# First tiles in halves, three issuing engines, and the constants behind the fifth tile, in a one-core hybrid encoder layer

## The chip, the cores and the metric

The kernel runs on one core of a Trainium2 chip. The metric is the device time of one execution in microseconds, as a median of several runs. The engines are TensorE (PE, with its weight loads as PEld), VectorE (DVE), ScalarE (ACT), GpSimd (POOL) and SyncE (SP, which issues most transfers). A row with "q" behind the engine (SPq, ACTq, POOLq) is the issue of a transfer.

## The reference

One layer for 512 positions of 1024 channels in float32. What the change touches is the very beginning: the norm, the input projection and the branch gates.

```python
def rms_norm(x, g):
    y = x32 * lax.rsqrt(jnp.mean(x32 * x32, axis=-1, keepdims=True) + EPS)
    return (y * g.astype(jnp.float32)).astype(x.dtype)
...
h = rms_norm(x, norm_mix[l])
proj = jnp.einsum('bsd,dc->bsc', h, w_in[l])
u_pool, u_lru, q, k, v, g_logits = jnp.split(proj, splits, axis=-1)
gates = jax.nn.sigmoid(g_logits + b_gate[l]).reshape(B, S, N_BRANCH, D_MODEL)
y_pool, y_lru = pool_mixer(u_pool, ...), rglru_mixer(u_lru, ..., lru_lambda[l])
y_sb = stick_breaking_attention(qh, kh, vh)      # after a norm of q and k by head
merged = (gates[:, :, 0] * jnp.einsum('bsc,cd->bsd', y_pool, w_branch[l, 0])
          + gates[:, :, 1] * jnp.einsum('bsc,cd->bsd', y_lru, w_branch[l, 1])
          + gates[:, :, 2] * jnp.einsum('bsc,cd->bsd', y_sb, w_branch[l, 2]))
x = x + jnp.einsum('bsd,de->bse', merged, w_out[l])
h2 = rms_norm(x, norm_ffn[l])
act = jax.nn.silu(h2 @ w_ffn_gate[l]) * (h2 @ w_ffn_up[l])
x = x + act @ w_ffn_down[l]
```

## The kernel before

Channels lie on the 128 partitions, positions (512) in the free dimension; the contraction of 1024 channels is done in eight tiles k of 128. Every float32 product is made of three matmuls: each operand is split into a rounded high part and the remainder, and high x high, high x low and low x high are added. Splitting takes a copy with rounding (on ScalarE, or a CAST on VectorE) and a subtraction on VectorE. For weights these parts are called `whi` and `wlo`, for the input `hu` holds both parts of x times the norm's weight (without the root of the mean square, which is applied later to the outputs).

The kernel begins with a gate projection of 512 columns. Its weights come as four `raw` tiles of two k each ("first", 0 to 3); `raw` has three buffers. `xt` is the transposed input, one tile of 128 x 512 for each k. Tile 0 of the weights is handled apart: `raw0` is loaded in two pieces, one for each k, and VectorE makes both parts (L451, L452). Tiles 1 to 3 go through `split_w` (ScalarE L111, VectorE L112). `make_h(k)` makes the parts of the input: ScalarE L437, VectorE L438, with the norm's weight taken as a column of `vt`. `vt` (128 x 114) holds every small constant of the layer, the norm's weights, biases and `lru_lambda` among them; it is loaded first. Meanwhile TensorE runs matmuls on a constant tile `warm` (L422). The gate matmuls are at L701: for each k, four column groups n for (whi, hu high), four for (wlo, hu high) and four for (whi, hu low).

`lru_constants` (L540 to L560) turns `lru_lambda` into two columns by a chain of some 25 tiny VectorE operations with one GpSimd power (L547) in it. `input_rms` loads the plain input `xs` and takes its squares on ScalarE. Both are written behind the first gate matmuls or later.

The order in which each engine's instructions stand is made by a scheduler from the program and its priorities, not by the written order alone: it is fixed at build time, and each engine has one list. A transfer also stands in the list of the engine that issues it, and waits there if the semaphore or buffer that it takes is not free.

Of the kernel before, what the change touches and what calls it, by code (L numbers as in the profile page):

```python
# [8 lines left out]
F32 = mybir.dt.float32  # L9
F32R = mybir.dt.float32r  # L10
BF16 = mybir.dt.bfloat16
AF = mybir.ActivationFunctionType
ALU = mybir.AluOpType
# [3 lines left out]
P = 128  # L17
S = 512
D = 1024
KT = D // P  # L20
# [4 lines left out]
HD = 128  # L25
QSCALE = float(HD) ** -0.5
EARLY = 300
WARM = 9
GBUFS = 27
NDIRECT = 2  # L30
KD = 10
NTICK = (1, 1)
H = S // 2
AHEAD = 200
PAD = 41


OFF = 16
# [11 lines left out]
VOFF = {}  # L50
# [17 lines left out]
def layer_kernel(ctx: ExitStack, tc: tile.TileContext, x, xt, vecs, w_in, w_qkv7, w_gate7, w_pool, w_rg, w_ig,  # L68
                 w_branch, w_br7, w_out, w_fg, w_fu, w_fd, w_fd7, out):
    nc = tc.nc  # L70
    act = nc.scalar.activation
    dve = nc.vector

    cst = ctx.enter_context(tc.tile_pool(name="cst", bufs=1))
# [18 lines left out]
    def cols(ap, k0, nk, c0, nc_):  # L93
        return ap[k0 * P:(k0 + nk) * P, c0:c0 + nc_].rearrange("(k p) c -> p k c", p=P)
# [5 lines left out]
    def weight_tiles(nh, nl, o=0):  # L100
        return [wp.tile([P, 1024 + 128], F32R, tag=tag, name=n)[:, o:o + 1024]
                for tag, n in (("whi", nh), ("wlo", nl))]
# [158 lines left out]
    def emit_next():  # L261
        i = state["i"]
        if i >= len(specs):
            return
        state["i"] = i + 1
        key, make = specs[i]
        with tc.high_priority(AHEAD if i > 6 else 0):
            ready[key] = make(str(i))

    def weights(*key):  # L270
        while key not in ready:
            emit_next()
        while len(ready) < 3 and state["i"] < state["stop"]:
            emit_next()
        return ready.pop(key)
# [16 lines left out]
    vt = cst.tile([P, NV], F32, tag="vt", name="vt")  # L292

    def vcol(name, i=0):
        o = VOFF[name] + i
        return vt[:, o:o + 1]


    cst.tile([P, PAD], F32, tag="pad", name="pad")
    warm = cst.tile([P, S], BF16, tag="warm", name="warm")  # L300
    dve.memset(warm, 1.0)
# [55 lines left out]
    def chunk_psum(key, pool, pair=False):  # L357
        nm = "ps_" + "_".join(map(str, key))
        if pool is None:
            return [pmm.tile([P, S], F32, tag="mm", name=nm + f"_{j}") for j in range(2)]  # L360
        t = pool.tile([P, 2, S], F32, tag="mm", name=nm)
        return t if pair else [t[:, j, :] for j in range(2)]


    def chan_chunk(key, rhs, nticks=0, pool=None, pair=False):
        pss = chunk_psum(key, pool, pair)
        for half in range(2):
            half_chunk(pss if type(pss) is list else [pss[:, j, :] for j in range(2)], key, half, rhs,
                       nticks)
        return pss  # L370
# [37 lines left out]
    with ExitStack() as first:  # L408
# [7 lines left out]
        def t4(shape, name, dt=F32):  # L416
            return b4(shape, name, "t", dt)


        wps = pb.tile([P, 2, S], F32, tag="mm", name="warm_ps")  # L420
        for i in range(WARM):
            nc.tensor.matmul(wps[:, 0, :], warm[:, 0:P], warm, start=True, stop=True)  # L422
# [4 lines left out]
        xts = [xp[k // 2][:, k % 2, :] for k in range(KT)]  # L427
        hu = []

        def load_xt(k):  # L430
            nc.sync.dma_start(xts[k], xt[k * P:(k + 1) * P, :])

        def make_h(k):
            t = t4([2, S], f"hu{k}", F32R)
            hh, hl = t[:, 0, :], t[:, 1, :]
            gcol = vcol("norm_mix", k)
            act(hh, xts[k], AF.Copy, scale=gcol)  # L437
            dve.scalar_tensor_tensor(hl, xts[k], gcol, hh.bitcast(F32), ALU.mult, ALU.subtract)  # L438
            hu.append((hh, hl))


# [1 line left out]
        hi0, lo0 = (t.rearrange("p (a b) -> p a b", a=2) for t in weight_tiles("whi0", "wlo0"))  # L443
        raw0 = wp.tile([P, 2, 512], F32, tag="raw", name="raw0")
        ready["first", 0] = hi0, lo0
        src0 = cols(w_in, 0, 2, 5120, 512)
        nc.sync.dma_start(vt, vecs)
        for k in range(2):
            load_xt(k)
            (nc.sync if k else nc.scalar).dma_start(raw0[:, k, :], src0[:, k, :])  # L450
            dve.tensor_copy(hi0[:, k, :], raw0[:, k, :])  # L451
            dve.tensor_tensor(lo0[:, k, :], raw0[:, k, :], hi0[:, k, :].bitcast(F32), ALU.subtract)  # L452
            make_h(k)
        load_xt(2)
        emit_next()
        make_h(2)
        load_xt(3)
        make_h(3)
        load_xt(4)
        emit_next()  # L460
        make_h(4)
        for k in range(5, KT):
# [11 lines left out]
        def input_rms():  # L474
            ssq = cst.tile([P, NS, 2], F32, tag="ssqa", name="ssqa")
            ms = cst.tile([P, NS], F32, tag="msa", name="msa")
            for sj in range(NS):
                t = w4([2, 512], f"xs{sj}")
                nc.sync.dma_start(t, x[sj * P:(sj + 1) * P, :].rearrange("p (e c) -> p e c", e=2))
                for ej in range(2):  # L480
                    act(t[:, ej, :], t[:, ej, :], AF.Square, accum_out=ssq[:, sj, ej:ej + 1])
            dve.tensor_tensor(ms, ssq[:, :, 0], ssq[:, :, 1], ALU.add)
            dve.tensor_scalar(ms, ms, 1.0 / D, EPS, ALU.mult, ALU.add)
            rsqrt(rx, ms, (NS,), "a")
# [210 lines left out]
        pss = [chunk_psum(("gate", 0, c), pb) for c in range(2)]  # L695
        for k in range(KT):
            if k % 2 == 0:
                wh, wl = weights("first", k // 2)
            for w, x_ in ((wh, 0), (wl, 0), (wh, 1)):
                for n in range(4):  # L700
                    nc.tensor.matmul(pss[n // 2][n % 2], w[:, k % 2, n * P:(n + 1) * P], hu[k][x_],  # L701
                                     start=k == 0 and w is wh and x_ == 0,
                                     stop=k == KT - 1 and x_ == 1)
            if k == 3:
                input_rms()
        bg.append(rms_broadcast)
# [146 lines left out]
        for cc in range(2):  # L853
# [14 lines left out]
            for nm in ORDER:  # L868
                ps, half, first_, t, ts_, src, ss = plan[nm]
# [314 lines left out]
    with ExitStack() as third:  # L1184
# [42 lines left out]
        for u, nm in BORDER:  # L1227
            z, half, first_, sn, ts_ = plan[nm]
# [5 lines left out]
            for w in range(2):  # L1234
                o = ps[:, w, half * H:(half + 1) * H]
                for k in range(4):
                    for n, (x_, y_) in enumerate(((0, 0), (0, 1), (1, 0))):
                        nc.tensor.matmul(o, ah[x_][:, w, k, :], b[k][y_], start=first_ and n == k == 0,  # L1238
                                         stop=n == 2 and k == 3, skip_group_check=True)
            if sn is not None:  # L1240
                if (u, sn) not in snaps:
                    snaps[u, sn] = ap2.tile([P, 2, S], F32, tag="t", name=f"bt{u}{sn}")
                with tc.high_priority(EARLY):
                    act(snaps[u, sn][:, :, ts_], ps[:, :, hi], AF.Copy,
                        scale=-1.0 if sn and (u, sn) in gated else 1.0)
# [10 lines left out]
    with ExitStack() as ffn:  # L1256
        gp = ffn.enter_context(tc.tile_pool(name="gp", bufs=GBUFS))

        def g4(shape, name, dt=F32):

            return gp.tile([P] + shape, dt, tag="g", name=name)
# [13 lines left out]
        for c in range(4):  # L1275
# [7 lines left out]
            pss = psh[c] if c < 2 else chan_chunk(("out", c), mt, pool=fp)  # L1283
            hh = g4([2, S], f"h2h{c}", F32R)
            hl = g4([2, S], f"h2l{c}", F32R)
            for j in range(2):
                k = 2 * c + j
# [5 lines left out]
                gcol = vcol("norm_ffn", k)  # L1293
# [272 lines left out]
        for e in range(2):  # L1566
            wh, wl = weights("fd", e)
# [4 lines left out]
            for j in range(4):  # L1572
                m = 4 * e + j
                cs = slice(j * P, (j + 1) * P)
# [117 lines left out]
```

## Time and profile before

| what | value |
|---|---|
| median of 3 runs | 898.24 us (898.1 to 898.4) |
| profiled execution, own time | 898.31 us |
| profiled execution, span | 896.5 us |
| TensorE busy | 891.2 us, 99% of the span |
| VectorE / ScalarE / GpSimd busy | 739.4 / 528.5 / 88.8 us |
| moved by DMA | 154.08 MB, mean 172 GB/s |

A row of the timeline has its start, its duration, engine, line, operation, output <- input, shapes, a count of merged instructions, and in brackets the idle time before it with what ended it. A row of the waits says who waited for whom: total, times, longest. A row of a stretch gives the busy time of TensorE, its weight loads, VectorE, ScalarE and GpSimd (instructions in brackets), the granted clock, the share of the DMA engines and their GB/s. A row of issues gives the size and the median time from issue to landing.

### The profile page before, as it was taken

How to read it: one execution, taken by the hardware profiler on the slowest of the kernel's cores; microseconds unless marked ns; L12 is line 12 of the kernel's file. 1: busy time of each engine (PE TensorE's matmuls, PEld its weight loads, DVE VectorE, ACT ScalarE, POOL GpSimd, SP SyncE). 2: the span in 40 equal slices, each digit the busy share in tenths (PEclk: the TensorE clock that was granted, in tenths of full speed). 3: DMA queues.
4: the chain of work that ended last, by engine and by line, in shares of the span. 5: the costliest groups of instructions: out<-in, count | busy, mean ns of one | idle time of the engine just before them, and what ended most of it. 6: DMA issues, size and time to landing. Idle time of an engine off the chain costs nothing.

```text
span 896.5 us, 14227 instructions
## 1 busy us (share of the span) xinstructions
PE 891.2 (99%) x5563; PEld 795.2 (89%) x5563; DVE 739.4 (82%) x934; ACT 528.5 (59%) x730; POOL 88.8 (10%) x130
## 2 busy tenths in 40 slices
PE   9999999999999999999999999999999999999998
PEld 6888778788889888888888988889999999999998
DVE  6897897997786599967887695699988888899974
ACT  6554989546856556554664544545555555746642
POOL 1110002222323101000001100000000000021200
PEclk9999999999999999999999999999999999999999
DMA  9495336798692785734636865336443343897913
GB/s 337 141 297 167 118 114 215 217 302 252 174 276 72 217 252 175 236 108 152 205 90 154 179 190 170 106 107 169 126 131 104 95 118 97 228 243 195 186 42 118
DMA packets 116644, 154.08 MB, mean 172 GB/s; under 512 B 8161, under 2 KB 90081, under 8 KB 116577
## 3 DMA queue, kind: packets, MB, share of 16 engines
q1 hardware_dynamic: 103904, 107.30, 37.8%
q0 software_dynamic: 12528, 45.62, 21.6%
q8 instruction: 43, 0.70, 0.3%
q10 hardware_dynamic: 144, 0.26, 0.1%
q14 instruction: 25, 0.20, 0.1%
HBM read 132.71 MB, written 18.87 MB: 169 GB/s over the span
## 4 chain that ended last, share of the span: by engine, by line
PE 95%; DVE 2%; ACT 2%; issue 1%; DMA 0%; SPq 0%; DVEq 0%; ACTq 0%
PE ps_y L287 11%; PE ps_x L287 8%; PE ps_q L798 7%; PE ps_dy L1611 6%; PE ps_dx L1611 5%; PE ps_br L278 3%; PE ps_br L279 3%; PE ps_br L280 3%; PE ps_bY L1238 2%; PE ps_gate L701 2%; PE ps_gy L287 2%; PE ps_gate L280 2%; PE ps_bX L1238 2%; PE ps_gx L287 2%; PE ps_gate L278 2%; PE ps_gate L279 2%
## 5 line engine op out<-in xcount | busy, mean ns | idle before, releaser
L111 ACT ACTIVATE whi<-raw 128x1024 fp32r<-128x1024 f32 x69 | 73.1, 1060 | 85.2 <-PE ps_out L279 17.9
L112 DVE TENSOR_TENSOR wlo<-raw,whi 128x1024 fp32r<-128x1024 f32 x69 | 84.4, 1223 | 30.7 <-ACT whi L111 30.7
L112 DVE TENSOR_TENSOR wlo<-qw,whi 128x1024 fp32r<-128x1024 f32 x48 | 58.6, 1224 | 22.0 <-ACT whi L111 21.8
L111 ACT ACTIVATE whi<-qw 128x1024 fp32r<-128x1024 f32 x48 | 50.7, 1059 | 33.2 <-PE ps_q L798 15.3
L1403 ACT ACTIVATE wh_S<-w_S 128x1024 fp32r<-128x1024 f32 x36 | 38.3, 1067 | 34.4 <-PE ps_y L287 22.3
L1404 DVE TENSOR_TENSOR wl_S<-w_S,wh_S 128x1024 fp32r<-128x1024 f32 x36 | 43.8, 1222 | 5.2 <-ACT wh_S L1403 5.1
L1515 POOL DMA_DIRECT2D dw<-in_w_down_dram x20 | 16.9, 847 | 313.6 <-DMA dw<-in_w_down_dram 253.2
L1403 ACT ACTIVATE wh<-w 128x1024 fp32r<-128x1024 f32 x27 | 28.8, 1067 | 30.2 <-issue 11.9
L1404 DVE TENSOR_TENSOR wl<-w,wh 128x1024 fp32r<-128x1024 f32 x27 | 33.0, 1222 | 9.9 <-ACT wh L1403 9.9
L1403 ACT ACTIVATE whdS<-dw 128x1024 fp32r<-128x1024 f32 x20 | 21.3, 1067 | 22.5 <-PE ps_dy L1611 11.0
L1404 DVE TENSOR_TENSOR wldS<-dw,whdS 128x1024 fp32r<-128x1024 f32 x20 | 24.3, 1226 | 6.5 <-ACT whdS L1403 6.4
L1054 DVE TENSOR_TENSOR_SCAN E<-K,ahead 128x512 f32<-128x512 f32 (+3 forms) x32 | 25.4, 815 | 4.4 <-ACT K L1050 4.4
L278 PE MATMUL ps_br<-yHH,whi 128*128 128x512 f32 x64 | 25.3, 395 | 0.0
L278 PE MATMUL ps_lru<-HH,whi 128*128 128x512 f32 x64 | 25.2, 394 | 0.0
L278 PE MATMUL ps_br<-yph,whi 128*128 128x512 f32 x64 | 25.2, 394 | 0.0
L278 PE MATMUL ps_pool<-HH,whi 128*128 128x512 f32 x64 | 25.2, 393 | 0.0
L280 PE MATMUL ps_gate<-HH,wlo 128*128 128x512 f32 x64 | 25.0, 391 | 0.0
L278 PE MATMUL ps_gate<-HH,whi 128*128 128x512 f32 x64 | 25.0, 391 | 0.0
L279 PE MATMUL ps_br<-ypl,whi 128*128 128x512 f32 x64 | 25.0, 391 | 0.0
L280 PE MATMUL ps_br<-yph,wlo 128*128 128x512 f32 x64 | 25.0, 391 | 0.0
L279 PE MATMUL ps_br<-yHL,whi 128*128 128x512 f32 x64 | 25.0, 390 | 0.0
L279 PE MATMUL ps_pool<-HL,whi 128*128 128x512 f32 x64 | 25.0, 390 | 0.0
(737 smaller groups left out, 3448.5 us busy)
## 6 DMA issues: line engine op xcount, KB each, us to landing
raw<-in_w_in_dram SPq DMA_DIRECT2D x31, 512.0 KB, 5.3
qw<-in_w_qkv_dram SPq DMA_DIRECT2D x24, 512.0 KB, 7.4
dw<-in_w_down_dram POOLq DMA_DIRECT2D x20, 512.0 KB, 7.5
w<-in_w_ffn_gate_dram SPq DMA_DIRECT2D x36, 256.0 KB, 4.0
w<-in_w_ffn_up_dram SPq DMA_DIRECT2D x36, 256.0 KB, 4.6
raw<-in_w_branch_dram SPq DMA_DIRECT2D x16, 512.0 KB, 4.1
qw<-in_w_qkv_dram POOLq DMA_DIRECT2D x12, 512.0 KB, 7.7
qd<-r POOLq DMA_DIRECT2D x12, 512.0 KB, 7.9
```

Source lines behind the costliest of these rows:

```text
L111: act(hi, raw, AF.Copy)
L112: dve.tensor_tensor(lo, raw, hi.bitcast(F32), ALU.subtract)
L278: nc.tensor.matmul(ps, lh, rh, start=start, stop=False, skip_group_check=skip)
L279: nc.tensor.matmul(ps, lh, rl, start=False, stop=False, skip_group_check=skip)
L280: nc.tensor.matmul(ps, ll, rh, start=False, stop=stop, skip_group_check=skip)
L287: nc.tensor.matmul(o, a_[a][:, w, k, :], b_[b][:, k, :], start=first and n == k == 0, stop=last and n == 2 and k == 3, skip_group_check=True)
L798: nc.tensor.matmul(ps[:, a, :], b_[:, k, ts_], a_[:, kk, :], start=first and n == k == 0, stop=n == 2 and k == 3, skip_group_check=True)
L1054: dve.tensor_tensor_scan(E[:, c0:c0 + n][:, ::-1], K[:, c0 + 1:c0 + n + 1][:, ::-1], ahead[:, S - n:][:, ::-1], 0.0, ALU.mult, ALU.add)
L1238: nc.tensor.matmul(o, ah[x_][:, w, k, :], b[k][y_], start=first_ and n == k == 0, stop=n == 2 and k == 3, skip_group_check=True)
L1403: act(h, src, AF.Copy)
L1404: dve.tensor_tensor(l, src, h.bitcast(F32), ALU.subtract)
L1611: nc.tensor.matmul(o, a_[a][:, w, k0 + k, :], b_[b][:, k, :], start=first and i == k == 0, stop=last and i == 2 and k == nk - 1, skip_grou ...
```

## The change

The norm's eight weight columns get a tile of their own, `nmix`, loaded first from the same array; the pad behind it shrinks by eight columns, so that the other constants keep their addresses. The first input tile and the first half of `raw0` are loaded in two column halves each, from SyncE and ScalarE; the second half of `raw0` (for k=1) is loaded whole, from GpSimd. The rounding of the weights, `make_h(0)` and the matmuls of k=0 work on halves too: 24 matmuls of 256 columns for 12 of 512. `vt` is loaded behind the fifth input tile. There are seven warming matmuls instead of nine.

```diff
-WARM = 9
+WARM = 7
-PAD = 41
+PAD = 33
+    nmix = cst.tile([P, 8], F32, tag="nmix", name="nmix")
...
-        def make_h(k):
+        def make_h(k, parts=(slice(0, S),)):
...
-            gcol = vcol("norm_mix", k)
-            act(hh, xts[k], AF.Copy, scale=gcol)
-            dve.scalar_tensor_tensor(hl, xts[k], gcol, hh.bitcast(F32), ALU.mult, ALU.subtract)
+            gcol = nmix[:, k:k + 1]
+            for ts_ in parts:
+                act(hh[:, ts_], xts[k][:, ts_], AF.Copy, scale=gcol)
+            for ts_ in parts:
+                dve.scalar_tensor_tensor(hl[:, ts_], xts[k][:, ts_], gcol, hh[:, ts_].bitcast(F32),
+                                         ALU.mult, ALU.subtract)
...
-        nc.sync.dma_start(vt, vecs)
-        for k in range(2):
-            load_xt(k)
-            (nc.sync if k else nc.scalar).dma_start(raw0[:, k, :], src0[:, k, :])
-            dve.tensor_copy(hi0[:, k, :], raw0[:, k, :])
-            dve.tensor_tensor(lo0[:, k, :], raw0[:, k, :], hi0[:, k, :].bitcast(F32), ALU.subtract)
-            make_h(k)
+        o = VOFF["norm_mix"]
+        nc.sync.dma_start(nmix, vecs[:, o:o + 8])
+        def round_first(k, cs):
+            dve.tensor_copy(hi0[:, k, cs], raw0[:, k, cs])
+            dve.tensor_tensor(lo0[:, k, cs], raw0[:, k, cs], hi0[:, k, cs].bitcast(F32), ALU.subtract)
+        HF = (slice(0, S // 2), slice(S // 2, S))
+        nc.scalar.dma_start(raw0[:, 0, HF[0]], src0[:, 0, HF[0]])
+        nc.sync.dma_start(xts[0][:, HF[0]], xt[0:P, HF[0]])
+        nc.scalar.dma_start(xts[0][:, HF[1]], xt[0:P, HF[1]])
+        nc.scalar.dma_start(raw0[:, 0, HF[1]], src0[:, 0, HF[1]])
+        load_xt(1)
+        nc.gpsimd.dma_start(raw0[:, 1, :], src0[:, 1, :])
+        for cs in HF:
+            round_first(0, cs)
+        make_h(0, HF)
+        round_first(1, slice(0, S))
+        make_h(1)
         load_xt(2)
         emit_next()
         make_h(2)
         load_xt(3)
         make_h(3)
         load_xt(4)
+        nc.sync.dma_start(vt, vecs)
         emit_next()
...
-            for w, x_ in ((wh, 0), (wl, 0), (wh, 1)):
-                for n in range(4):
-                    nc.tensor.matmul(pss[n // 2][n % 2], w[:, k % 2, n * P:(n + 1) * P], hu[k][x_],
...
+            for ns, ts_ in [(ns, ts_) for ns in ((0, 1), (2, 3)) for ts_ in HF] if k == 0 else \
+                    (((0, 1, 2, 3), slice(0, S)),):
+                for w, x_ in ((wh, 0), (wl, 0), (wh, 1)):
+                    for n in ns:
+                        nc.tensor.matmul(pss[n // 2][n % 2][:, ts_], w[:, k % 2, n * P:(n + 1) * P],
+                                         hu[k][x_][:, ts_],
...
```

The change also gives the scheduler another program, and each engine's list comes out in another order. VectorE, from the `warm` memset on; a number behind a name is a buffer's, `raw_136`, `whi_134` and `wlo_135` are tile 0 before (two halves, k=0 at L451 first, k=1 at the second L451), `lt` are the small tiles of `lru_constants`. Before:

```order
L301 MEMSET warm 128x512
L540 TENSOR_SCALAR qg<-vt 128x1
L544 TENSOR_SCALAR lt_475<-vt 128x8
L545 TENSOR_TENSOR lt_477<-lt_475,vt 128x8
L451 CAST whi_134<-raw_136 128x512
L557 TENSOR_SCALAR lt_475<-lt_475 128x8
L452 TENSOR_TENSOR wlo_135<-raw_136,whi_134 128x512
L438 SCALAR_TENSOR_TENSOR hu_142<-xt_130,vt,hu_142 128x512
L438 SCALAR_TENSOR_TENSOR hu_149<-xt_130,vt,hu_149 128x512
L451 CAST whi_134<-raw_136 128x512
L452 TENSOR_TENSOR wlo_135<-raw_136,whi_134 128x512
```

Now, from the input tiles k=1 (`hu_154`) and k=2 (`hu_164`) on; `raw_135`, `whi_133` and `wlo_134` are tile 0, whose k=0 halves (128x256) stand ahead of these rows; `raw_158` and `wlo_161` are raw tile 1, `hu_168` and `hu_179` the fourth and fifth input tile:

```order
L443 SCALAR_TENSOR_TENSOR hu_164<-xt_130,nmix,hu_164 128x512
L112 TENSOR_TENSOR wlo_161<-raw_158,whi_160 128x1024
L443 SCALAR_TENSOR_TENSOR hu_168<-xt_130,nmix,hu_168 128x512
L443 SCALAR_TENSOR_TENSOR hu_179<-xt_131,nmix,hu_179 128x512
L560 TENSOR_SCALAR qg<-vt 128x1
L564 TENSOR_SCALAR lt_493<-vt 128x8
L565 TENSOR_TENSOR lt_495<-lt_493,vt 128x8
L577 TENSOR_SCALAR lt_493<-lt_493 128x8
L568 TENSOR_SCALAR lt_496<-lt_495 128x8
L457 CAST whi_133<-raw_135 128x512
L569 RECIPROCAL lt_496<-lt_496 128x8
L458 TENSOR_TENSOR wlo_134<-raw_135,whi_133 128x512
```

The CAST and the subtraction for k=1 (the 128x512 ones) have moved from before raw tile 1 to behind it, behind two input tiles, behind the first operations on `vt`, and behind L568, which takes the result of the GpSimd power.

SyncE's first transfers, before:

```order
L447 DMA vt<-in_vecs_dram 128x114
L431 DMA xt_130<-in_xt_dram 128x512 x2
L450 DMA raw_136<-in_w_in_dram 128x512
L431 DMA xt_131<-in_xt_dram 128x512
L118 DMA raw_153<-in_w_in_dram 128x2x512
L431 DMA xt_131<-in_xt_dram 128x512
L431 DMA xt_132<-in_xt_dram 128x512
L118 DMA raw_167<-in_w_in_dram 128x2x512
```

and now:

```order
L454 DMA nmix<-in_vecs_dram 128x8
L463 DMA xt_129<-in_xt_dram 128x256
L434 DMA xt_129<-in_xt_dram 128x512
L434 DMA xt_130<-in_xt_dram 128x512
L118 DMA raw_158<-in_w_in_dram 128x2x512
L434 DMA xt_130<-in_xt_dram 128x512
L434 DMA xt_131<-in_xt_dram 128x512
L479 DMA vt<-in_vecs_dram 128x114
L118 DMA raw_173<-in_w_in_dram 128x2x512
```

`vt` has gone from the first to the eighth place, and the half of `raw0` for k=1 has left this list for GpSimd's, where it stands behind the five constants' memsets and ahead of the sixteen `invpos` ones. On TensorE the gate matmuls of k=0 are halved and partly interleaved; those of k=1 and after stand as before.

More of the change, by code (lines that the diff above doesn't have):

```diff
@@ L698, in layer_kernel @@
                 wh, wl = weights("first", k // 2)
-            for w, x_ in ((wh, 0), (wl, 0), (wh, 1)):
-                for n in range(4):
-                    nc.tensor.matmul(pss[n // 2][n % 2], w[:, k % 2, n * P:(n + 1) * P], hu[k][x_],
-                                     start=k == 0 and w is wh and x_ == 0,
-                                     stop=k == KT - 1 and x_ == 1)
+            for ns, ts_ in [(ns, ts_) for ns in ((0, 1), (2, 3)) for ts_ in HF] if k == 0 else \
[4 more added lines that the diff above has]
+                                         hu[k][x_][:, ts_],
+                                         start=k == 0 and w is wh and x_ == 0 and ts_ == HF[0],
+                                         stop=k == KT - 1 and x_ == 1, skip_group_check=True)
             if k == 3:
```

## The prediction

> **What bounds the kernel now.** I read the page first (busy shares, then the chain that ended last), then who waited for whom on TensorE, then the first 30 us row by row, because every line of the change works there.
>
> ```profile
> span 896.5 us, 14227 instructions
> PE 891.2 (99%) x5563; PEld 795.2 (89%) x5563; DVE 739.4 (82%) x934; ACT 528.5 (59%) x730; POOL 88.8 (10%) x130
> PE 95%; DVE 2%; ACT 2%; issue 1%; DMA 0%; SPq 0%; DVEq 0%; ACTq 0%
> PE warm_ps L422 <- DVE warm L301: 1.5, 1, 1.5
> PE ps_q L798 <- DVE wlo L112: 0.4, 1, 0.4
> PE ps_gate L701 <- ACT hu L437: 0.3, 1, 0.3
> ```
>
> TensorE is busy for 891.2 of 896.5 us and carries 95% of the chain. The last three rows are all its waits of any size. So the kernel is TensorE's list of matmuls, and a microsecond that TensorE loses or gains at the start arrives at the end nearly whole, unless some slack takes it up. The start looks like this on TensorE:
>
> ```profile
> 1.46 3.97 PE L422 MATMUL warm_ps<-warm 128*128 128x512 bf16 x9 [1.46 <-DVE warm L301]
> 5.70 1.20 PE L701 MATMUL ps_gate<-hu,whi 128*128 128x512 f32 x4 [0.27 <-ACT hu L437]
> 6.73 1.07 PE L701 MATMUL ps_gate<-hu,wlo 128*128 128x512 f32 x4
> 7.64 1.98 PE L701 MATMUL ps_gate<-hu,whi 128*128 128x512 f32 x8
> 9.46 1.07 PE L701 MATMUL ps_gate<-hu,wlo 128*128 128x512 f32 x4
> 5.70 22.05 PE ps_gate L701 x96
> ```
>
> Nine warming matmuls fill the time until the first tile is there, then 96 gate matmuls (8 tiles k of 12) run without a hole. From 6.73 to 7.64 four start: 0.227 us each, 2.72 us a tile. Tile k=1 starts four matmuls after 7.64, at 8.55.
>
> **The part that brings something.** Two warming matmuls fewer, and first transfers of half the size, can let the first real matmul start when the seven warming ones end: 1.46 + 7 x 0.43 (the spacing that 3.97 us for nine shows) = about 4.5, against 5.70: up to 1.2 us earlier. The halved matmuls of k=0 (24 of 256 columns for 12 of 512) cost nothing in themselves:
>
> ```profile
> 651.05 0.28 PE L287 MATMUL ps_y<-B0T4l,wh 128*128 128x256 f32 x1
> 651.17 0.28 PE L287 MATMUL ps_y<-B0T4h,wl 128*128 128x256 f32 x1
> ```
>
> 256 columns start every 0.11 us, half of 0.227. So k=0 would be finished between 7.3 and 7.8.
>
> **The part that costs.** The gain only counts if tile k=1 is ready by then. Its weights are the second half of `raw0`, rounded on VectorE by a CAST (0.42 us) and a subtraction. Before, VectorE came to this CAST at 7.29. In the changed order it is VectorE's seventeenth instruction after the `warm` memset: behind the subtraction of raw tile 1, behind `hu3` and `hu4` (the fourth and fifth input tile), behind the first operations on `vt`, which is now loaded after the fifth tile, and behind L568, which waits for the GpSimd power (`lru_constants` of the code, now L560 to L580). Here is what those steps took before:
>
> ```profile
> 3.94 0.15 DVE L540 TENSOR_SCALAR qg<-vt 128x1 f32<-128x1 f32 x1 [2.54 <-DMA vt<-in_vecs_dram]
> 4.01 0.16 DVE L544 TENSOR_SCALAR lt<-vt 128x8 f32<-128x8 f32 x1
> 4.29 0.42 DVE L451 CAST whi<-raw 128x512 fp32r<-128x512 f32 x1
> 4.53 1.72 POOL L547 TENSOR_TENSOR lt<-lt,lt 128x8 f32<-128x8 f32 x1 [2.48 <-DVE lt L545]
> 4.92 0.72 ACT L437 ACTIVATE hu<-xt,vt 128x512 fp32r<-128x512 f32 x1 [2.14 <-DMA xt<-in_xt_dram]
> 7.29 0.42 DVE L451 CAST whi<-raw 128x512 fp32r<-128x512 f32 x1
> 8.94 0.75 DVE L438 SCALAR_TENSOR_TENSOR hu<-xt,vt,hu 128x512 fp32r<-128x512 f32 x1 [0.50 <-ACT hu L437]
> 9.60 0.17 DVE L548 TENSOR_SCALAR lt<-lt 128x8 f32<-128x8 f32 x1
> 9.62 1.06 ACT L111 ACTIVATE whi<-raw 128x1024 fp32r<-128x1024 f32 x1 [0.72 <-DMA raw<-in_w_in_dram]
> 10.72 1.23 DVE L112 TENSOR_TENSOR wlo<-raw,whi 128x1024 fp32r<-128x1024 f32 x1 [0.51 <-ACT whi L111]
> 11.86 1.41 DVE L438 SCALAR_TENSOR_TENSOR hu<-xt,vt,hu 128x512 fp32r<-128x512 f32 x2
> 13.18 0.16 DVE L551 TENSOR_TENSOR lt<-lt 128x8 f32<-128x8 f32 x1
> 22.67 1.01 POOL L315 TENSOR_TENSOR rsqa<-msa,mhalf 128x4 f32<-128x4 f32 x1 [16.42 <-DVE msa L483]
> 23.71 0.16 DVE L316 TENSOR_TENSOR rx<-rsqa 128x4 f32<-128x4 f32 x1 [1.12 <-POOL rsqa L315]
> ```
>
> VectorE takes its instructions in the order written: L548 needed only the power, done at 6.25, and yet ran at 9.60, after everything ahead of it. [...]
>
> Now the sum for the CAST of k=1. Raw tile 1 landed at 9.62; its rounding and subtraction and the two `hu` behind it let the next VectorE instruction start at 13.18. In the changed order that next one is `qg<-vt`. From `qg` to the start of the power 0.59 (3.94 to 4.53), the power 1.72, from its end to VectorE 0.03 (22.67 + 1.01 to 23.71), L568 to the next independent instruction 0.07 (3.94 to 4.01), the CAST 0.42, and 0.06 to the matmul (ScalarE ended at 5.64, TensorE started at 5.70): 2.89. So k=1 starts at 13.18 + 2.89 = 16.07 instead of 8.55: **7.5 us later**. Its low half follows at once (0.69 us of subtraction inside the 0.91 us of the first four matmuls). SyncE issues raw tile 1 sooner: one full transfer fewer stands ahead of it (0.45 us of issue), the 57 KB of `vt` are gone from its head, but `raw0`'s half now competes from GpSimd's queue:
>
> ```profile
> 3.07 0.43 SPq L118 DMA_DIRECT2D raw<-in_w_in_dram  x1
> 4.56 0.61 SPq L118 DMA_DIRECT2D raw<-in_w_in_dram  x1
> 5.21 1.80 SPq L431 DMA_DIRECT2D xt<-in_xt_dram  x3
> 10.00:15.00 5.00, 5.00 (x24) 4.14 (x23) 4.32 (x11) 4.58 (x7) 0.00 (x0) 1.00 1.05 401
> DMA to landing us min/median/max: 3.6/6.7/7.8
> DMA to landing us min/median/max: 3.4/6.7/9.3
> vt<-in_vecs_dram SPq DMA_DIRECT2D x1, 57.0 KB, 3.2
> ```
>
> The DMA engines are full (share 1.05 at 401 GB/s), so bytes count, not issue times: between 0 and 1.1 us earlier (0.45 plus 256 KB at 401 GB/s, 0.65). I take 0.3, nearer the full-engine end. `vt` itself is issued eighth on SyncE, near 5 us. As slow as the median input tile, 6.7 (the first row of landings is `xt`'s, the second `raw`'s), it lands at 11.7, before VectorE asks at 12.9: hidden.
>
> **The clock.** TensorE would be idle from about 7.5 to 15.8. No row shows a hole in the middle, so the price lies between 0 and that of the one start from idle in the trace: nine warming matmuls in 3.97 us where the later spacing gives 9 x 0.227 = 2.04, so 1.9 lost. Eight idle microseconds resemble that start more than the 0.27 us before 5.70, after which the matmuls ran at full rate; I take 1.9. (The granted-clock column shows 1.00 throughout and tells nothing here.) [...]
>
> **What else moves.** With k=1 done, k=2 to k=5 have their data since long. Raw tile 3 needs the buffer that the late subtraction frees (about 16.9), and the four `xs` loads are queued behind it on SyncE. Even with 9.3, the longest landing of a weight tile, it is there at 26.2, while k=6 starts after 16 + 5 x 2.72 = 29.6; ScalarE's 1.06 and VectorE's 1.23 fit between. The `xs` (2 MB, 5.2 us at 401 GB/s) shift by about as much as TensorE, so the broadcast of the norm is as ready as before. `nmix`, the ACT-issued halves and `make_h`'s four half instructions (two for one on each engine) lie in the hole. The GpSimd issue costs that engine under a microsecond where it is idle. Beyond 27 us the order is the same but for a few transfers; TensorE's waits there, under 1 us in the first fence, are no slack to win back 7.
>
> **Sum.** The profiled execution took 898.31 (0.07 above the median 898.24). + 7.5 - 0.3 + 1.9 = 907.4; on the median's scale **907.3 us**.
>
> **Rivals.**
> *The hole, but a warm clock.* If TensorE resumes at full rate: 898.24 + 7.2 = 905.4. For it: nothing in the trace shows the rate falling; against: the start from idle. Chance 0.22.
> *`vt` later still.* The longest landing of a weight tile was 9.3; from an issue near 5 that is 14.3, 1.4 behind VectorE's turn, and all of it is added: 908.7. For it: full engines and 456-byte rows; against: 57 KB landed in 3.2 at the start. Chance 0.14.
> *Faster: k=1 is ready in time.* TensorE starts 1.2 us earlier and no hole opens: 897.1. The CAST begins 13.18 - 9.62 + 2.41 = 6.0 us after raw tile 1 lands, and would have to begin by 6.8 (7.3 less 0.42 and 0.06): raw tile 1 landed by 0.8, before any weight has been moved. It turns on this one point, and the full engines speak against it. Chance 0.04.
> *The edit does little, since the hole is refilled.* If later slack gave back nearly all: 898.2. Against: the TensorE waits above sum to 2.2 us, 1.8 of them before 6 us. Chance 0.04.
>
> **Numbers.** The forecast has 0.56. Three cases (0.92) end slower; measurement here tells about 0.2% (1.8 us) from no change, and all three lie beyond 905. Range: low end 904.5 (warm clock and raw tile 1 1.1 us earlier: 898.24 + 7.5 - 1.1 = 904.6), high end 909.5 (`vt` late, no earlier landing, 898.24 + 7.5 + 1.9 + 1.4 = 909.0, and a little for a longer warming). Faster 0.04, same 0.04, slower 0.92.
>
> **What would show it.** In the changed profile: gate matmuls of k=0 starting at 4.5 to 4.9; then TensorE waiting some 8 us at L724 for VectorE's CAST at L457; on VectorE, `qg` at about 12.9, idle until the power ends, the 128x512 CAST near 15.4; matmuls of 0.43 us spacing behind the hole, then 0.227. A CAST before 10 would make the prediction wrong, as would a power that starts before 9, or a TensorE that never waits after k=0.

## The result and the profile after

The changed kernel takes 907.86 us, the median of five runs (907.06 to 908.44); the kernel before, on the same chip, 898.24 (898.06 to 900.62). The ratio is 1.0104, with a 95% interval of 1.0093 to 1.0115: 9.6 us slower. The forecast was 907.3 us in 904.5 to 909.5. The profiled execution is the fastest of the five: 907.06 us, 8.75 more than the one before (898.31).

The head of the page, busy time and chain, of the changed kernel:

```profile
span 905.3 us, 14256 instructions
PE 894.8 (99%) x5573; PEld 798.3 (88%) x5573; DVE 739.6 (82%) x937; ACT 527.7 (58%) x731; POOL 90.2 (10%) x131
PE 92%; DVE 3%; ACT 2%; DMA 2%; issue 1%; SPq 0%; POOL 0%; DVEq 0%; ACTq 0%; POOLq 0%
```

The span grew by 8.8, but TensorE's busy time only by 3.6, so more than half of the loss is time in which TensorE stood still. In the chain TensorE gave up three points, taken by VectorE and DMA; that share does not measure the loss, since the kernel of the ninth experiment, as fast as the one before, also has PE 93% and DMA 2%. From TensorE's waits in the changed kernel (who waited for whom: total, times, longest):

```profile
PE ps_gate L724 <- DVE lt L569: 3.4, 1, 3.4
PE ps_gate L724 <- DVE whi L457: 1.6, 1, 1.6
...
PE pq L1042 <- DMA at<-qd: 0.2, 1, 0.2
```

Two waits are new, both in the first gate matmuls (L724): 1.6 us inside k=0 and 3.4 in front of k=1. The start row by row, all engines together:

```profile
4.64 0.61 PE L724 MATMUL ps_gate<-hu,whi 128*128 128x256 f32 x2
5.08 0.40 PE L724 MATMUL ps_gate<-hu,wlo 128*128 128x256 f32 x2
...
6.70 0.29 DVE L457 CAST whi<-raw 128x256 fp32r<-128x256 f32 x1 [2.97 <-DMA raw<-in_w_in_dram]
7.05 0.50 PE L724 MATMUL ps_gate<-hu,whi 128*128 128x256 f32 x2 [1.56 <-DVE whi L457]
...
8.51 1.06 ACT L111 ACTIVATE whi<-raw 128x1024 fp32r<-128x1024 f32 x1 [0.63 <-DMA raw<-in_w_in_dram]
9.60 1.22 DVE L112 TENSOR_TENSOR wlo<-raw,whi 128x1024 fp32r<-128x1024 f32 x1
10.95 0.63 PE L724 MATMUL ps_gate<-hu,whi 128*128 128x256 f32 x2
12.06 0.14 DVE L560 TENSOR_SCALAR qg<-vt 128x1 f32<-128x1 f32 x1
12.64 1.67 POOL L567 TENSOR_TENSOR lt<-lt,lt 128x8 f32<-128x8 f32 x1 [9.81 <-DVE lt L565]
14.35 0.17 DVE L568 TENSOR_SCALAR lt<-lt 128x8 f32<-128x8 f32 x1 [1.66 <-POOL lt L567]
14.43 0.42 DVE L457 CAST whi<-raw 128x512 fp32r<-128x512 f32 x1
15.00 1.92 PE L724 MATMUL ps_gate<-hu,whi 128*128 128x512 f32 x4 [3.42 <-DVE lt L569]
16.72 1.91 PE L724 MATMUL ps_gate<-hu,wlo 128*128 128x512 f32 x4
18.43 2.05 PE L724 MATMUL ps_gate<-hu,whi 128*128 128x512 f32 x8
20.31 1.07 PE L724 MATMUL ps_gate<-hu,wlo 128*128 128x512 f32 x4
```

Read upward from 15.00. The CAST of k=1 (14.43) has no wait of its own; it stands behind L568, which waited 1.66 us for the GpSimd power, which waited for `vt`'s operations, which stand behind the subtraction of raw tile 1 (9.60) and two `hu`. The bracket at 15.00 names L569, a small operation that VectorE ran right behind the CAST and that ended last; the data that the matmul reads is the CAST's. Were the transfers late? The changed kernel's issues (KB each, median us from issue to landing):

```profile
raw<-in_w_in_dram POOLq DMA_DIRECT2D x1, 256.0 KB, 4.7
raw<-in_w_in_dram ACTq DMA_DIRECT2D x2, 128.0 KB, 3.6
vt<-in_vecs_dram SPq DMA_DIRECT2D x1, 57.0 KB, 5.9
```

GpSimd issued its transfer at 1.51, so the weights of k=1 lay there at 6.2 and waited 8.2 us for VectorE. `vt`, issued at 4.18, was there at 10.1, before `qg` asked at 12.06. Neither was late; the order of VectorE's list was.

Stretches of this execution of the changed kernel, cut where the granted clock changed (TensorE, its weight loads, VectorE, ScalarE, GpSimd; granted clock, DMA share, GB/s):

```profile
4.89:8.30 3.41, 1.83 (x10) 1.27 (x11) 1.57 (x5) 1.49 (x3) 0.00 (x0) 1.00 1.03 392
8.30:11.71 3.41, 3.28 (x16) 2.98 (x15) 3.38 (x5) 2.55 (x4) 0.00 (x0) 0.50 1.05 379
11.71:15.13 3.42, 0.13 (x1) 0.16 (x2) 1.69 (x9) 2.63 (x4) 1.67 (x1) 1.00 1.05 372
15.13:18.54 3.41, 3.41 (x9) 2.64 (x10) 3.41 (x5) 0.72 (x2) 0.00 (x0) 0.50 1.02 407
```

The clock goes in steps of 3.41 us: full, half, full, half, and full from 18.54 on. Each half step follows one in which TensorE had stood idle for much of the time (busy 1.83 and 0.13 of 3.41), the full ones follow steps that were busy (3.28, 3.41). So the full step granted from 11.71 falls into the hole and is wasted (0.13 of 3.42 us used), and k=1 meets the half step behind it, from 15.13. The pattern is not the same in every execution: the mean granted clock is 0.995 to 0.997 in four of the five, 1.000 in the one of 908.38.

The same broadcast of the norm stands in both chains, first before, then after:

```profile
30.47 0.89 PE rbps L492 x8
```

```profile
38.61 0.89 PE rbps L512 x8
```

So 8.14 us are lost by there, nearly all that the profiled execution lost: k=1 starts at 15.00 instead of 8.55 (6.45), and its twelve matmuls take 15.00 to 19.40 (20.31 less four of 0.227), 4.40 instead of 2.72 (1.68).

### The profile page after: what moved, and what is told of

Read it like the earlier page. It is cut to its first block, busy times and chain, and to the rows that moved or that the text cites. A ratio compares the mean times of both kernels' runs of the same rounds, so it can differ in the third digit from the quotient of the medians.

```text
span 905.3 us, 14256 instructions
## 1 busy us (share of the span) xinstructions
PE 894.8 (99%) x5573; PEld 798.3 (88%) x5573; DVE 739.6 (82%) x937; ACT 527.7 (58%) x731; POOL 90.2 (10%) x131
## 4 chain that ended last, share of the span: by engine, by line
PE 92%; DVE 3%; ACT 2%; DMA 2%; issue 1%; SPq 0%; POOL 0%; DVEq 0%; ACTq 0%; POOLq 0%
PE ps_y L287 11%; PE ps_x L287 8%; PE ps_q L822 7%; PE ps_dy L1635 6%; PE ps_dx L1635 5%; PE ps_br L278 3%; PE ps_br L279 3%; PE ps_br L280 3%; PE ps_bY L1262 2%; PE ps_gate L724 2%; PE ps_gy L287 2%; PE ps_gate L280 2%; PE ps_bX L1262 2%; PE ps_gate L279 2%; PE ps_gate L278 2%; PE ps_lru L278 2%
## 5 line engine op out<-in xcount | busy, mean ns | idle before, releaser
L280 PE MATMUL ps_pool<-HH,wlo 128*128 128x512 f32 x64 | 25.0, 391 | 0.0
L280 PE MATMUL ps_br<-yHH,wlo 128*128 128x512 f32 x64 | 25.0, 390 | 0.0
```

The lines of the kernel that those rows point to most:

```text
L280: nc.tensor.matmul(ps, ll, rh, start=False, stop=stop, skip_group_check=skip)
```

## The experiments

Times are medians with their range; "before" in the same comparisons took 898.49, 898.29 and 898.39. "k=1" is the start of the first matmul of tile k=1 (8.55 before), and the shift is that of `rbps` against 30.47. Starts, waits and shifts are those of the one traced execution; where it lay far from the median, its own time is given.

### Before, with the second half of `raw0` issued from GpSimd

```diff
-            (nc.sync if k else nc.scalar).dma_start(raw0[:, k, :], src0[:, k, :])
+            (nc.gpsimd if k else nc.scalar).dma_start(raw0[:, k, :], src0[:, k, :])
```

> The kernel before with one word changed: the second half of raw0 (for k=1) is loaded from GpSimd. Theory (the scheduler puts the CAST of that half behind raw tile 1 and two more input tiles, so the list and not the transfer makes TensorE wait): CAST of k=1 at 12.9 to 13.5 us, its idle time not ended by the transfer, k=1 on TensorE at 13.4 to 14.0 instead of 8.55, then about 1.7 us of half rate: 904.5 to 905.5 us. Rival A (the transfer from GpSimd itself lands late): the CAST waits for that transfer. Rival B (the late vt is the whole cause): 898.2 us, as before.

Measured: 906.3 us (904.91 to 906.61), ratio 1.0086 [1.0073, 1.0100]; shift 7.47. Its timeline:

```profile
7.49 1.07 PE L701 MATMUL ps_gate<-hu,whi 128*128 128x512 f32 x4
...
12.88 0.38 DVE L451 CAST whi<-raw 128x512 fp32r<-128x512 f32 x1
13.40 2.05 PE L701 MATMUL ps_gate<-hu,whi 128*128 128x512 f32 x4 [4.84 <-ACT hu L437]
...
19.65 1.07 PE L701 MATMUL ps_gate<-hu,wlo 128*128 128x512 f32 x4
```

One word makes most of the change's loss, without halves, without a late `vt`, and with nine warming matmuls. The CAST of k=1, at 7.29 before, runs at 12.88 with no wait for its data, behind raw tile 1, two `hu` and L548 (at 12.56), the order of the changed kernel. (The bracket at 13.40 names ScalarE's `hu`, which had long been done: the wait was for the CAST.) The delay is 13.40 - 8.55 = 4.85, and the half rate costs 2.62 more: twelve matmuls until 18.74 (19.65 less 0.91), 5.34 instead of 2.72. Its stretches at the same steps:

```profile
8.54:11.95 3.41, 0.02 (x1) 0.00 (x0) 2.42 (x4) 2.52 (x4) 0.00 (x0) 1.00 1.05 399
11.95:15.36 3.41, 1.96 (x5) 1.41 (x6) 3.38 (x9) 2.65 (x4) 0.00 (x0) 0.50 0.97 318
15.36:18.77 3.41, 3.41 (x10) 2.64 (x10) 3.12 (x12) 0.72 (x2) 0.00 (x0) 0.50 1.02 417
```

Here k=0 ran at full rate to its end (6.57 to 7.49 for four, 0.23 apart), the step with 0.02 us of matmuls was followed by one at 0.50, and so was the next one, busy for only 1.96: two half steps instead of the one that I expected, and so 0.8 more than my 905.5. Here a wait of 4.84 us stood ahead of the half rate; in the changed kernel a wait of only 1.56 us, with the rate full (two matmuls of 256 columns in 0.40 from 5.08 on), was already followed by a half step (the stretch from 8.30 on).

### The changed kernel, with that half issued from SyncE

```diff
-        nc.gpsimd.dma_start(raw0[:, 1, :], src0[:, 1, :])
+        nc.sync.dma_start(raw0[:, 1, :], src0[:, 1, :])
```

> The changed kernel with one word changed: the k=1 half of raw0 is loaded from SyncE. Theory (the GpSimd issue made the hole, through the order): no wait above 1 us at k=1, but the late second quarter of raw0 (6.7 us in the changed kernel) and a cold clock still make k=0 end near 10.9 instead of 8.55: 900 to 901 us. Rival A (halves bring the early start that they promise): 897 us. Rival B (late vt makes the hole): still 906 us or more.

Measured: 900.1 us (898.82 to 902.61; the traced execution 900.6), 1.0018 [1.0009, 1.0027]; shift 2.08. Its timeline on TensorE:

```profile
4.55 0.80 PE L724 MATMUL ps_gate<-hu,whi 128*128 128x256 f32 x2
...
10.18 1.50 PE L724 MATMUL ps_gate<-hu,whi 128*128 128x256 f32 x6
11.52 1.08 PE L724 MATMUL ps_gate<-hu,wlo 128*128 128x512 f32 x4
```

The hole is gone: the issuing engine accounts for 8.14 - 2.08 = 6.06 us of the shift (by the medians, 8.0 of the 9.6). What stays is a new cost: k=0 starts 1.15 us earlier than before and ends later. Most of its 24 half matmuls ran 0.213 us apart, twice the 0.11 that the prediction took, until k=1 at 10.61 (10.18 + 2 x 0.213): by this spacing TensorE was still at half rate.

### The changed kernel, with `vt` in front again

```diff
         nc.sync.dma_start(nmix, vecs[:, o:o + 8])
+        nc.sync.dma_start(vt, vecs)
...
         load_xt(4)
-        nc.sync.dma_start(vt, vecs)
```

> The changed kernel with vt loaded second, right behind nmix; GpSimd still loads the k=1 half. Theory (the wait for the power on late constants is the last 2 us of the hole): the CAST of k=1 follows the fifth input tile at once, k=1 starts near 13.2 instead of 15.0: 906.0 us, 1.8 under the changed kernel. Rival A (vt's place does not matter): as the changed kernel, 907.9. Rival B (vt's place is the whole cause): 900 us or less.

Measured: 904.09 us (903.97 to 904.79), 1.0068 [1.0055, 1.0082]; shift 5.20. Its timeline:

```profile
7.31 0.80 PE L724 MATMUL ps_gate<-hu,whi 128*128 128x256 f32 x2 [2.68 <-ACT hu L441]
...
13.06 0.42 DVE L458 CAST whi<-raw 128x512 fp32r<-128x512 f32 x1
13.63 1.17 PE L724 MATMUL ps_gate<-hu,whi 128*128 128x512 f32 x4 [0.89 <-DVE lt L569]
```

The power no longer makes VectorE wait, but the CAST still comes only at 13.06, behind raw tile 1. So `vt` in front takes 2.94 off the 8.14 (8.14 - 5.20), more than the 1.8 that I expected. Of it 1.37 is the earlier start (15.00 to 13.63). The other 1.55 is the clock: k=0 ran late (from 7.31) and without a hole, only 0.89 of idle time remained in front of k=1, and k=1's first four matmuls took 1.00 us (13.63 to 14.63) instead of 1.72.

### The changed kernel, with eight warming matmuls in the hole

```diff
+            if k == 1:
+                for i in range(8):
+                    tc.keep_in_program_order(nc.tensor.matmul(wps[:, 0, :], warm[:, 0:P], warm, ...))
```

> The changed kernel with eight more matmuls on the constant tile between k=0 and k=1 on TensorE, which fill most of the hole (8 x 0.43 us = 3.4). Theory (the idle time costs the clock on top of the wait): k=1 starts at 15.0 as before but its 12 matmuls take 2.7 us, not 4.4: 1.7 us less, 906.2 us. Rival (the slow matmuls behind the hole have another cause, such as operands still being written): no gain, 907.9 us.

Measured: 906.5 us (905.26 to 906.89), 1.0089 [1.0075, 1.0103]; shift 7.72. Its timeline:

```profile
7.82 0.29 DVE L457 CAST whi<-raw 128x256 fp32r<-128x256 f32 x1 [4.06 <-DMA raw<-in_w_in_dram]
...
16.16 1.17 PE L727 MATMUL ps_gate<-hu,whi 128*128 128x512 f32 x4 [0.82 <-DVE lt L569]
17.17 1.08 PE L727 MATMUL ps_gate<-hu,wlo 128*128 128x512 f32 x4
```

The clock term is shown: behind the filler k=1's first four matmuls took 1.01 us instead of 1.72. In the medians the gain is 1.4 us, of the 1.7 expected. The traced execution (906.89, the longest of the four) hardly gained, because in it the second quarter of `raw0` landed 1.12 later (7.82 against 6.70), VectorE's list with it, and k=1 started at 16.16.

### The changed kernel, with VectorE's list pinned in the written order

```diff
-                dve.scalar_tensor_tensor(hl[:, ts_], ...)
+                pin(dve.scalar_tensor_tensor(hl[:, ts_], ...), 1 <= k <= 4)
...
-            dve.tensor_scalar(qg, vcol("q_norm"), QSCALE, None, ALU.mult)
+            tc.keep_in_program_order(dve.tensor_scalar(qg, vcol("q_norm"), QSCALE, None, ALU.mult))
... (and so for the subtractions of raw tiles 1 and 2 and the first operation on lru_lambda)
```

> The changed kernel with all its transfers (GpSimd still loads the k=1 half of raw0), but VectorE's list pinned in the written order: the CAST and subtraction of k=1 straight behind k=0's parts, then raw tile 1, the input tiles and raw tile 2, the constants made from vt much later. Theory (order, not the GpSimd transfer, made the hole): CAST of k=1 by 9 us, no hole; k=0 still slow as in the SyncE variant, 900 to 901 us. Rival (the GpSimd transfer or its queue is late): the CAST waits for the transfer beyond 10 us, 903 us or more.

Measured: 901.98 us (901.51 to 903.71; the traced execution 903.34), 1.0045 [1.0032, 1.0057]; shift 4.12. Its timeline:

```profile
7.20 0.80 PE L730 MATMUL ps_gate<-hu,whi 128*128 128x256 f32 x2 [1.32 <-DVE whi L463]
8.32 0.43 DVE L463 CAST whi<-raw 128x512 fp32r<-128x512 f32 x1
...
11.43 2.28 PE L730 MATMUL ps_gate<-hu,whi 128*128 128x256 f32 x6
```

The transfer is still GpSimd's, and the CAST of k=1 runs at 8.32, again without a wait for data. Together with the first experiment this settles it: not the transfer but the place that the scheduler gave its consumer made the hole. Why the scheduler chose that place was not examined. The time missed my 900 to 901 by a microsecond. The trace has the cost that the second experiment showed: the 1.32 us wait for the second quarter (landed at 6.85), and half rate through k=0 (0.21 us apart from 9.08 on) and into k=1 (the last two of k=0 and the first four of k=1, 2.28 us).

### Warming, apart from the rest

Three runs ask what the start itself is worth. The second experiment's kernel with ten warming matmuls instead of seven:

> The changed kernel with the k=1 half from SyncE, and ten warming matmuls instead of seven. Theory (what is left of the loss without the hole, 2.0 us at 30 us, is k=0 running at half rate, because seven warming matmuls and the gaps behind them never fill the time that the clock asks for): gate matmuls of k=0 start at 5.8 and run at or near full rate, k=1 starts near 9: 898.2 to 899.2 us. Rival (the halves or the late second quarter cost the 2 us, not the clock): no better than with seven, 900 us, or 901 since the start is a microsecond later.

Measured: 899.99 us (899.38 to 901.18; the traced execution 900.75), 1.0018 [1.0009, 1.0027]; shift 0.99. And the kernel before with seven instead of nine, nothing else:

> The kernel before with seven warming matmuls instead of nine and nothing else. Theory (clock): TensorE is idle from 4.6 to 5.7 and the first gate matmuls then run at 0.43 us each for 3 us or more: 1.5 to 3 us more, 899.7 to 901 us. Rival (a microsecond of idle time costs nothing there): 898.2 us.

Measured: 900.04 us (897.93 to 901.09; the traced execution is the longest of the eleven), 1.0013 [1.0005, 1.0022]; shift 2.30. TensorE in the first of these two, then in the second:

```profile
5.31 0.40 PE L724 MATMUL ps_gate<-hu,wlo 128*128 128x256 f32 x2
7.02 0.75 PE L724 MATMUL ps_gate<-hu,whi 128*128 128x256 f32 x4 [1.31 <-DVE hu L443]
```

```profile
5.65 2.07 PE L701 MATMUL ps_gate<-hu,whi 128*128 128x512 f32 x4 [1.02 <-ACT hu L437]
```

With seven, the list and the transfers of before are untouched and the first real matmul starts where it did (5.65 against 5.70), yet behind the 1.02 us of idle time in front of it the rate is half through most of k=0 (2.07 for the first four, 1.20 before), and k=1 starts at 10.82, 2.27 late. With ten, the rate was full from 5.31 on (0.40 for two of 256 columns; 0.63 in the second experiment), and behind the 1.31 us of idle time that followed it was full again (7.83 to 8.31 for four, 0.12 apart). So two of the change's own lines, fewer warming matmuls and an input that comes in pieces, cost more than the earlier start gives. With ten, the trace ended 1.1 us sooner than the second experiment's (897.7 against 898.8), about half of what my theory expected; the time stayed, and missed my 898.2 to 899.2: in its runs 1.7 to 3.1 us lie outside the span (3.05 in the traced one), in all others here 1.7 to 1.9. Why stays open.

The kernel before, with `vt` issued from ScalarE behind `raw0`'s first half, so that the input leaves SyncE first:

```diff
-        nc.sync.dma_start(vt, vecs)
...
+            if k == 0:
+                nc.scalar.dma_start(vt, vecs)
```

> The kernel before with vt issued from ScalarE behind the first half of raw0, so that SyncE's first transfer is the first input tile; whole tiles, nine warming matmuls. Theory (only the landing of whole first tiles sets the start): the input tile lands 0.3 to 0.5 earlier, the gate matmuls start at 5.45 when the warming ones end, 0.25 us less: 898.0 us, not to be told from 898.2 by time, but by the start of k=1 (8.3 instead of 8.55). Rival (the table load that moves back on ScalarE, or vt, is late): start after 5.7, 898.5 us or more.

Measured: 900.05 us (898.85 to 901.17), 1.0018 [1.0009, 1.0027]; shift 2.73. Its timeline:

```profile
5.46 1.34 ACT L437 ACTIVATE hu<-xt,vt 128x512 fp32r<-128x512 f32 x2 [2.19 <-DMA vt<-in_vecs_dram]
6.24 2.08 PE L702 MATMUL ps_gate<-hu,whi 128*128 128x512 f32 x4 [0.76 <-ACT hu L437]
```

The rival won: `vt`, second on its queue, took 4.2 us to land instead of 3.2, ScalarE waited for it, and the start moved back by 0.54 with a hole of 0.76, behind which the rate was again half (2.08 us for the first four).

### The part of the change that costs nothing

The kernel before with `nmix` in front and `vt` behind the fifth tile, without halves, without GpSimd, nine warming matmuls:

```diff
-        nc.sync.dma_start(vt, vecs)
+        nc.sync.dma_start(nmix, vecs[:, o:o + 8])
...
         load_xt(4)
+        nc.sync.dma_start(vt, vecs)
```

> The kernel before with only the move of the constants: nmix loaded first and used by make_h, vt loaded behind the fifth input tile; whole first tiles, nine warming matmuls, no GpSimd transfer. Theory (the late constants cost only where other work stands behind them on VectorE; here the CAST of k=1 stands ahead of them): VectorE waits for the power near 12.5 to 14.3 but TensorE does not; the first input tile lands a little earlier, the start is 5.45 to 5.6 and the clock is up: 897.9 to 898.4 us, no change. Rival (late constants delay raw tile 2's subtraction behind them): TensorE waits at k=4 (about 17 us) and the time is 899 us or more.

Measured: 898.5 us (897.59 to 898.86), 0.9998 [0.9990, 1.0007]; shift -0.41. The same with ten warming matmuls:

> The same with ten warming matmuls, so that TensorE has no idle time before the first gate matmul (they end at 5.2 to 5.8). Theory (a start without idle time keeps the clock up in every execution): 898.0 to 898.5 us with a narrow spread, gate matmuls at full rate from the first. Rival (the tenth only delays): 898.7 us or more, by the 0.2 to 0.4 that the start is later.

Measured: 898.13 us (897.52 to 898.86), 0.9997 [0.9988, 1.0006]; shift -0.33. The timeline of the first:

```profile
5.28 1.19 PE L705 MATMUL ps_gate<-hu,whi 128*128 128x512 f32 x4 [0.31 <-ACT hu L439]
...
14.40 0.17 DVE L552 TENSOR_SCALAR lt<-lt 128x8 f32<-128x8 f32 x1 [1.66 <-POOL lt L551]
```

VectorE waits the same 1.66 us for the power as in the changed kernel, and nobody waits for VectorE: the CAST of k=1 is already past (7.27). The matmuls start 0.42 and 0.61 earlier (5.28 and 5.09) at full rate (1.03 and 1.01 us for the first four), 0.3 to 0.4 of it is still there at `rbps`, and in the time it is too small to be told from nothing. No version beat the kernel before by what can be measured.

## Why the prediction was right, and where its terms were off

**The cause: right.** The CAST of k=1 stood behind `vt` and the power, with its data there 8 us early; the one-word edit and the pinned list show that the list made the hole.

**The delay of k=1 (forecast 7.5 less 0.3, measured 6.45).** The term that was mis-sized is "I take 0.3": raw tile 1 landed at 8.5, 1.1 earlier, which was the far end of the bounds 0 to 1.1, not the near one. From `qg` to k=1 it went as worked out: 15.00 - 12.06 = 2.94 against 2.89.

**The clock (forecast 1.9, measured 1.68).** Right in kind and nearly in size: behind the filler the rate was full (1.01 us for four, not 1.72), so the warm-clock rival fell. The row that I took (the start from idle) was 0.2 too high; one step of 3.41 us at half rate (15.13 to 18.54) loses half of it, 1.7. The granted-clock column, which said nothing in the profile before, shows every step in the changed kernel from 4.89 on.

**k=0 (forecast finished at 7.3 to 7.8, measured about 11.4).** Wrong in two places. The second quarter of `raw0`, third on ScalarE's queue, landed at 6.7, 5.0 us after its issue, and TensorE waited 1.56 for it. And the 0.11 us for 256 columns was read from a row at full rate, while from 8.30 on TensorE had half of it. In the changed kernel the hole covers both, so TensorE waited 1.6 + 3.4 us instead of some 8 at once; without the hole (second experiment) they cost about 2 us. The sum did not suffer from this miss, since k=1 waited for the CAST either way.

**`vt` hidden, slack gives nothing back.** `vt` landed at 10.1 (forecast 11.7), hidden. The shift of 8.14 at `rbps` was not won back; it is 8.38 at the last VectorE operation (893.41 to 901.79), and the output adds 0.4 to the span. TensorE waits 0.2 in the attention for a load, as it did not before; the kernel before with only seven warming matmuls waits the same 0.2 there, and the second experiment's does not, so it does not take the moved transfers to make it.

**The sum.** By its terms the forecast was 9.1, the trace had 8.13 of them at `rbps`; the median came to 9.6 because of the later 0.6 and because the profiled execution was 0.8 under its median. Part of the near agreement is thus luck: a delay forecast 0.75 too large and a clock term 0.2 too large were made up for by 1.4 us that no term of the sum had.

## What to carry to other kernels

When a transfer moves to another issuing engine, read the consumer's place in its engine's list before and after: the data came early, and the list cost 6 us. At the start of a kernel, keep TensorE busy without a gap up to the first real matmul: 1.02 us of idle time there put k=1 back by 2.27 us here, more than the 1.15 by which the smaller first tile started sooner. Price a short instruction at the rate that TensorE has at that place (256 columns: 0.213 us apart at the start), not at that of the same instruction later (0.11 at 651 us).

## What the runs showed of the hardware

That the granted clock moves in steps of 3.41 us, and that the rate of each goes with how busy the one before was, I had not expected to see so plainly: in the changed kernel and in the first experiment the steps were full behind 3.28, 3.41 and 3.41 us of matmuls, half behind 1.83, 0.13, 0.02 and 1.96. The half rate behind a short hole lasted longer than a step: idle time of 1.02 us (seven warming matmuls) and 0.76 (`vt` from ScalarE) at the start was followed by some 5 us of it, while 0.31 at 5.28 (the ninth), 0.89 (`vt` in front) and 1.31 with the rate full (ten warming matmuls) were followed by full rate; 1.56 in the changed kernel, also with the rate full, was followed by a half step. Where the steps lie differs from run to run (counted back by 3.41, an edge lies at 1.48 in the changed kernel, at 1.71 in the first experiment's, near 0.5 in the one with seven warming matmuls, there from the estimate below). That fits the spread of the kernel with seven warming matmuls, 897.93 to 901.09, where the kernel before had 897.78 to 899.41, but no run here shows that it is the cause. How busy a step must be is open: 1.96 of 3.41 did not give the rate back, but in the second experiment TensorE was idle for only 0.2 us before 10 and still stayed at half rate until 10.6.

The granted-clock column can mislead at the start. In the kernel with seven warming matmuls it reads, from the first gate matmul on:

```profile
5.65:10.60 4.95, 4.95 (x12) 3.88 (x13) 3.72 (x8) 2.46 (x4) 0.53 (x1) 1.00 1.03 377
```

Twelve matmuls in 4.95 us is 0.41 apart, nearly half rate, beside a granted clock of 1.00. By the rows the full rate came near 10.7 (an estimate: eight matmuls in the 2.50 us from 9.23 to 11.73, at first 0.43 apart, then 0.227). In the changed kernel the trace's first record of the clock is at 4.89; ahead of it the column reads 1.00 as well, while the warming matmuls ran 0.43 apart, and only the spacing tells the rate.

The same small load can also land at quite different times under full DMA engines (share 1.04 at 387 GB/s from 5 to 10 in the changed kernel): `raw0`'s second quarter, 128 KB and third on ScalarE's queue, was there at 6.70, 5.61, 6.92, 7.82 and 6.85 in five of these traces. The first, fourth and fifth have the same transfers in the same order (the changed kernel, the filler, the pinned list) and still differ by 1.1.
